# One shared transposed block for the two key triangles of the second query block in a sliding-window attention (float32 decoder trunk)

## The chip, the cores and the metric

The kernel runs on one core of a Trainium2 chip. The metric is the device time of one execution in microseconds (us). Four engines compute: TensorE (PE, matrix products and transposes, with PEld for its weight loads), VectorE (DVE), ScalarE (ACT) and GpSimd (POOL). SyncE (SP) and the queues of ACT and POOL start DMA transfers. The engines run on their own instruction streams, in order, and wait for one another through semaphores.

## The reference, cut to what matters

Two layers; each normalises the stream (256 tokens of 1024 channels), makes one wide input projection, runs three token mixers side by side (a state-space scan, a sliding-window attention with sinks, a forgetting attention), projects and gates each, merges, projects out and adds to the stream. The change is in the sliding-window attention:

```python
SWA_HEADS = 16; SWA_KV_HEADS = 4; HEAD_DIM = 64; SWA_WINDOW = 128; SWA_BLOCK = 128
def sliding_window_branch(q, k, v, z, sinks, cos, sin):
    ...                                   # rope on q and k; two query blocks of 128
    scores = jnp.einsum('bnqkgd,bnskd->bnkgqs', qb, kb).astype(jnp.float32) * (HEAD_DIM ** -0.5)
    diff = qi + blk - sj                  # sj runs over the block before and the own block
    band = (diff >= 0) & (diff < SWA_WINDOW)
    mask = band[None] & (key_pos >= 0)
    scores = jnp.where(mask[None, :, None, None], scores, -jnp.inf)
    ...                                   # the sink is one more column of the softmax
    probs = jax.nn.softmax(jnp.concatenate([scores, sink], axis=-1), axis=-1)[..., :-1]
    out = jnp.einsum('bnkgqs,bnskd->bnqkgd', probs.astype(v.dtype), vb)
    return out.reshape(b, s, SWA_HEADS * HEAD_DIM) * jax.nn.silu(z)
```

With a window of 128 and blocks of 128, query i of the second block sees key j of the block before if j > i, and key j of its own block if j <= i. The two sets of places (i, j) are the two triangles of one 128x128 square, and together they fill it once.

## The kernel before, in words

Products of the wide projections are made in float32r from weights split into a high and a low part: ACT rounds the high part (line 291), DVE subtracts for the low part (line 292), and PE multiplies (line 106). The weight pieces stream through six raw buffers and six split buffers; at most four split parts are held ahead. So the bulk of PE's work is dense products, and the mixers are fitted between them.

The order of PE's work is written by the program itself. Each mixer is a generator. Where it has to wait for other engines, it yields a number of microseconds of PE work (`D_SOFT = 7.0` after the scores, `D_SOFT2 = 3.0` between the two halves of the transposes, `D_EVAC = 3.0` after them). At the end of each dense unit (8 weight tiles against 256 tokens, or a token block against up to 512 columns) the function `pump` looks for generators whose time has come, by a planner's clock, and lets them issue their next step. Steps thus fall on the ends of dense units. The instructions of the other engines are put in order by the scheduler of the tile framework.

Sliding attention: one generator `swa_quad` for each of the four key-value groups of a layer, with four query heads each. It calls `attn_quad`, which the forgetting attention (`fox_quad`) uses too. For a quad, PE makes the scores; DVE adds the mask and takes the row minimum (line 615); ACT takes the exponential with the row sum (line 621); DVE scales each row (line 633). A quad holds two tiles `pp` of [128, 2 heads, 384]: columns 0 to 127 are the first query block, columns 128 to 383 the second query block with its two key blocks. Then PE transposes twelve 128x128 blocks (line 647, recorded at line 110), three for each head, into PSUM tiles of four blocks, ACT copies each tile to SBUF (line 652), and PE multiplies by the values. Only one quad is between its scores and the end of its transposes at a time (`tokens["pp"]`), and the value products of two quads are made together. A state-space group (`ssd_group`) begins when no quad of the sliding attention is left: `yield lambda: not any(m[2] == 1 for m in waiting)`; its first step starts a DMA of decay sums (line 808). The projection of the attention's output begins with `drain`, which runs all steps of that branch that are left.

GpSimd adds the rotated halves of queries and keys (lines 565 and 566), starts the DMAs that add the two parts of a product in SBUF (`dma_sum`, line 492), and masks the bias of the forgetting attention with `affine_select` (line 991). That bias arrives by a DMA that ACT starts (line 984), and its two buffers are shared with the values of the sliding attention.

Of the kernel before, what the change touches and what calls it, by code (L numbers as in the profile page):

```python
# [14 lines left out]
ALU = mybir.AluOpType  # L15

P = 128
S = 256
# [6 lines left out]
D_SOFT, D_SOFT2, D_EVAC, D_SSD, D_SSD2 = 7.0, 3.0, 3.0, 8.0, 4.0  # L25
D_K, D_Q, D_QK, D_G0, D_FOX, D_BDMA, D_BIAS, D_BC, D_SSD3 = 6.0, 5.5, 2.0, 8.0, 0.0, 4.0, 2.6, 5.5, 1.0
D_GN1, D_GN2, D_CUM, D_H, D_M = 8.0, 13.5, 12.0, (4.8, 6.4), 5.0
BUDGET = 1.35
T_PP, T_SSD, T_BIAS = 1, 1, 1
N_RAW, N_SPLIT = 6, 6  # L30
AHEAD = 4
WARM = 7
# [15 lines left out]
def hybrid_trunk(  # L48
# [5 lines left out]
    nc = tc.nc  # L54
# [11 lines left out]
    def T(tag, shape, dtype=F32, bufs=None):  # L66
        count[0] += 1
        return sb.tile(shape, dtype, tag=tag, name=f"{tag}_{count[0]}",
                       bufs=bufs if bufs is not None else BUFS.get(tag, 1))
# [8 lines left out]
    def pmx():  # L78
        return PS("mx", 5)
# [5 lines left out]
    gtt = nc.gpsimd.tensor_tensor  # L85
# [14 lines left out]
    def mm(o, a, b, **kw):  # L100
        n = b.free_size()
        if a.dtype == F32R:
            clock["t"] += max(0.094, n / 2350.0)
        else:
            clock["t"] += max(0.2, n / 587.0) * (0.5 if a.free_size() == 64 or a.shape[0] == 32 else 1.0)
        nc.tensor.matmul(o, a, b, **kw)  # L106

    def transpose(o, a, i):
        clock["t"] += 0.109
        nc.tensor.transpose(o, a, i)  # L110
# [74 lines left out]
    for j in range(2):  # L185
# [6 lines left out]
                            pattern=[[1, P]], channel_multiplier=-1)  # L192
# [3 lines left out]
                            pattern=[[1, P]], channel_multiplier=-1)  # L196
# [9 lines left out]
                            compare_op=ALU.is_ge, fill=NEG, base=0,  # L206
                            pattern=[[-1, P]], channel_multiplier=1)
    nc.gpsimd.affine_select(out=wmask[:, 0:P], in_=wmask[:, 0:P],
                            compare_op=ALU.is_ge, fill=NEG, base=-1,
                            pattern=[[1, P]], channel_multiplier=-1)  # L210
# [7 lines left out]
    def bc(ap, axis, n):  # L218
        s = list(ap.shape)
        s.insert(axis, n)  # L220
        return ap.unsqueeze(axis).to_broadcast(s)
# [204 lines left out]
    for l in range(L):  # L426
        y = Layer()
# [151 lines left out]
    def u_bq(y, g):  # L579

        def done(held):
            q = T("qt", [P, 2, S])
            add_rotated(q, held)
            launch(1, swa_quad(y, g, q), D_Q)
        return rotated(y, done)

    def attn_quad(y, last, products, biases, nsink, v, vcols, sz, gated, scored=lambda: None):

        yield Half("pp")
        pair = y.pair
        if y.values:
            yield Half(lambda: y.values[0] is not None)
            y.values.pop()()
        pps = [T("pp", [P, 2, 3 * P]) for _ in range(2)]
        nm = T("nm", [P, 8], bufs=2)
        sums = T("sums", [P, 8], bufs=2)
        blocks = ((0, slice(0, P)), (1, slice(P, 3 * P)))  # L600

        scs = [pmx() for _ in range(4)]

        def score(p, i, b):
            return scs[2 * p + i][:, b * P:P + 2 * P * b]

        products(score)
        for p in range(2):
            pp = pps[p]
            ps_ = slice(4 * p, 4 * p + 4)  # L610
            ns = None if nsink is None else nsink(p)
            for i in range(2):
                for b, sl in blocks:
                    e = 4 * p + 2 * i + b
                    nc.vector.tensor_tensor_reduce(  # L615
                        out=pp[:, i, sl], in0=score(p, i, b), in1=biases(p, i, b), scale=-0.125,
                        scalar=1.0e30 if ns is None else ns[:, i:i + 1],
                        op0=ALU.add, op1=ALU.min, accum_out=nm[:, e:e + 1])
                for b, sl in blocks:
                    e = 4 * p + 2 * i + b  # L620
                    act(pp[:, i, sl], pp[:, i, sl], AF.Exp, scale=-1.0, bias=nm[:, e:e + 1],  # L621
                        accum_out=sums[:, e:e + 1])
            if nsink is not None:
                es = T("es", [P, 4], bufs=2)
                tt(es.rearrange("p (i b) -> p i b", i=2), nm[:, ps_].rearrange("p (i b) -> p i b", i=2),
                   bc(ns, 2, 2), op=ALU.subtract)
                act(es, es, AF.Exp)
                tt(sums[:, ps_], sums[:, ps_], es, op=ALU.add)
            rs = T("rsum", [P, 4], bufs=4)
            nc.vector.reciprocal(rs, sums[:, ps_])  # L630
            for i in range(2):
                for b, sl in blocks:
                    ts(pp[:, i, sl], pp[:, i, sl], rs[:, 2 * i + b:2 * i + b + 1], 0.5,  # L633
                       op0=ALU.mult, op1=ALU.mult)
        yield D_SOFT
        scored()

        order = [(0, 0), (0, 1), (1, 0), (1, 1), (0, 2), (1, 2),
                 (2, 0), (2, 1), (2, 2), (3, 0), (3, 1), (3, 2)]
        at = {hb: (n // 4, n % 4 * P) for n, hb in enumerate(order)}  # L640
        pTs = []
        for n, (h, b) in enumerate(order):
            if n == 6:
                yield D_SOFT2
            if n % 4 == 0:
                pt = pmx()
            transpose(pt[:, n % 4 * P:(n % 4 + 1) * P], pps[h // 2][:, h % 2, b * P:(b + 1) * P], ident)
            if n % 4 == 3:
                if n == 3:
                    two = T("L4", [P, 2, 512])  # L650
                pT = T("L2", [P, 512]) if n == 11 else two[:, n // 4, :]
                act(pT, pt, AF.Copy)  # L652
                pTs.append(pT)
        yield D_EVAC
        tokens["pp"] += 1

        def products_with_values(bank):
            py = bank()
            for p in range(2):
                for b, o in ((0, 0), (1, P)):  # L660
                    for i in range(2):
                        n, c = at[2 * p + i, 2 * b]
                        mm(py[64 * i:64 * i + 64, S * p + o:S * p + S], v[:, b, vcols(p, i)],
                           pTs[n][:, c:c + S - o], start=(b == 0), stop=(b == 1))
            return py


        pair.append((gated, products_with_values, sz))
        if len(pair) == 2:
            quads = pair[:]  # L670
            pair.clear()

            def values():
                for py, (_, _, own) in zip([f(bank) for (_, f, _), bank in zip(quads, (pmx, pmm))], quads):
                    o = own()
                    tt(o, py.rearrange("p (u s) -> p u s", u=2), o, op=ALU.mult)
            if not last:
                y.values.append(None)
            gates = lambda: all(g() for g, _, _ in quads)
            yield Half(gates) if last else gates  # L680
            if last:
                values()
            else:
                y.values[0] = values

    def swa_quad(y, g, q):
        yield lambda: 1 in y.sz

        def products(score):
            for b in range(2):  # L690
                for c in range(2):
                    for h in range(4):
                        r = slice(32 * h, 32 * h + 32)
                        mm(score(h // 2, h % 2, b), q[r, c, b * P:(b + 1) * P], y.kT[r, (h - g) % 4, c, 0:(b + 1) * P],
                           start=(c == 0), stop=(c == 1))

        yield from attn_quad(
            y, g == 3, products, lambda p, i, b: wmask[:, P:2 * P] if b == 0 else wmask,
            lambda p: y.nsink[:, 4 * g + 2 * p:4 * g + 2 * p + 2], y.bv,
            lambda p, i: slice(64 * g, 64 * g + 64),  # L700
            lambda: y.sz[1][:, 2 * g:2 * g + 2, :], lambda: (1, 2 * g + 1) in y.zdone)


    def logits(y, t, i, p):
# [273 lines left out]
    def fox_quad(y, j):  # L978
# [26 lines left out]
        def scored():  # L1005
            tokens["bias"] += 1

        yield from attn_quad(y, j == 6, products, lambda p, i, b: bs[p][:, i, P * b:P + 2 * P * b], None, y.cv,
                             lambda p, i: slice(P * (j + p) + 64 * i, P * (j + p) + 64 * i + 64),
                             lambda: y.sz[2][:, j:j + 2, :], lambda: (2, j + 1) in y.zdone, scored)  # L1010
# [188 lines left out]
    for y in layers:  # L1199
# [10 lines left out]
        def cols(c0, n=256):  # L1210
            return sub([(0, w[:, c0:c0 + n])], n)
# [39 lines left out]
        if l == 0:  # L1251
            v, cv0, cv1 = cols(C_BV), cols(C_CV), cols(C_CV + 256)
# [8 lines left out]
        else:  # L1261
            cv0, v = cols(C_CV, 512), cols(C_BV)
# [87 lines left out]
    with tc.manual_schedule(engines={ENG.PE, ENG.DVE, ENG.Activation, ENG.Pool}):  # L1350
# [11 lines left out]
        p = pmx()  # L1362
# [93 lines left out]
        for i in range(2):  # L1456
# [4 lines left out]
        v = T("sm", [P, 8])  # L1461
        nc.vector.tensor_reduce(v[:, 0:2], ss.rearrange("p (t j) -> p t j", t=2), axis=mybir.AxisListType.X,
                                op=ALU.add)
# [50 lines left out]
```

## Time and profile before

| | |
|---|---|
| median of 3 runs | 821.57 us (821.18 to 821.93) |
| the profiled execution, its own time | 820.72 us |
| its span, first to last instruction | 819.0 us |
| mean granted TensorE clock | 0.999 |
| PE, PEld busy | 808.4 us (99%), 721.2 us (88%) |
| DVE busy | 671.5 us (82%) |
| ACT busy | 547.6 us (67%) |
| POOL busy | 172.6 us (21%) |

The table's busy times are shares of the whole span. The time outside the span is 1.72 us. Instructions of a helper all carry the helper's line: products line 106, transposes line 110. In the profile's names "x6" is a count, "<-" names what ended a wait, and tiles are called by their tags (`mm` and `mx` are PSUM tiles).

### The profile page before, as it was taken

Reading aid. Unit: us, or ns where it says so; the run is one execution under the profiler, and the core shown is the slowest. Engines: PE = TensorE matmul, PEld = TensorE weight load, DVE = VectorE, ACT = ScalarE, POOL = GpSimd, SP = SyncE. Lnnn points to the kernel's source line nnn. Section 1 sums busy time; section 2 is a strip of 40 time slices with the busy share of each in tenths; the row PEclk is TensorE's granted clock in tenths of the full one; section 3 lists DMA queues with packets and bytes.
Section 4 is the critical chain, followed back from the end, with each engine's and each line's share of the span. In section 5 each row is a group of like instructions: output and inputs, shape, how many; then the busy total and the mean of one; then the engine's idle time right before and its main releaser. Section 6 shows DMA issues by size and latency. Waiting matters only on the chain.

```text
span 819.0 us, 15070 instructions
## 1 busy us (share of the span) xinstructions
PE 808.4 (99%) x5242; PEld 721.2 (88%) x5242; DVE 671.5 (82%) x1468; ACT 547.6 (67%) x1186; POOL 172.6 (21%) x232
## 2 busy tenths in 40 slices
PE   8999999999999999999999999999999999999996
PEld 8998988888888988888999898889888889888896
DVE  6879899888998787965786989988899878787665
ACT  7777878775776767543666777886567767684452
POOL 3066113130210001030005621314004210102100
PEclk9999999999999999999999999999999999999999
DMA  9897869797865554866689787869868565467632
GB/s 312 278 261 193 211 187 256 190 233 214 232 206 157 180 168 148 276 208 205 221 265 265 186 222 206 228 179 259 243 206 231 155 181 163 137 208 265 206 104 77
DMA packets 141653, 170.35 MB, mean 208 GB/s; under 512 B 9314, under 2 KB 110298, under 8 KB 141578
## 3 DMA queue, kind: packets, MB, share of 16 engines
q1 hardware_dynamic: 114960, 140.53, 54.8%
q0 software_dynamic: 12928, 12.63, 9.5%
q10 hardware_dynamic: 13690, 16.24, 6.5%
q8 instruction: 41, 0.67, 0.3%
q14 instruction: 34, 0.28, 0.1%
HBM read 154.63 MB, written 2.16 MB: 191 GB/s over the span
## 4 chain that ended last, share of the span: by engine, by line
PE 85%; DVE 4%; DMA 4%; ACT 4%; issue 2%; POOL 0%; SPq 0%; ACTq 0%; DVEq 0%; POOLq 0%
PE mm L106 75%; PE mx L106 7%; PE mx L110 3%; DMA L<-cumd 2%; DVE lo L292 1%; ACT hi L291 1%; DVE L L781 1%; ACT pp L621 1%; DMA L<-L 1%; DMA raw<-in_w_in_dram 1%; DMA bias<-cumd 1%; ACT L L778 0%; ACT L L490 0%; DVE L L830 0%; POOL bias L991 0%
## 5 line engine op out<-in xcount | busy, mean ns | idle before, releaser
L292 DVE TENSOR_TENSOR lo<-raw,hi 128x1024 fp32r<-128x1024 f32 (+2 forms) x276 | 310.5, 1144 | 53.2 <-ACT hi L291 50.5
L106 PE MATMUL mm<-L,hi 128*128 128x512 f32 x1056 | 353.2, 386 | 0.0
L106 PE MATMUL mm<-hi,L 128*128 128x512 f32 (+2 forms) x1232 | 323.3, 351 | 0.1
L291 ACT ACTIVATE hi<-raw 128x1024 fp32r<-128x1024 f32 (+2 forms) x276 | 263.9, 981 | 57.2 <-PE mm L106 45.2
L106 PE MATMUL mm<-L,lo 128*128 128x256 f32 x1056 | 266.6, 273 | 0.0
L106 PEld LDWEIGHTS mm<-hi,L 128*128 128x128 f32 x1232 | 216.9, 190 | 24.1 <-issue 1.3
L106 PEld LDWEIGHTS mm<-L,hi 128*128 128x128 f32 x1056 | 194.5, 190 | 26.4 <-issue 3.2
L106 PE MATMUL mm<-lo,L 128*128 128x512 f32 (+2 forms) x616 | 213.8, 349 | 1.8 <-DVE lo L292 1.8
L106 PEld LDWEIGHTS mm<-L,lo 128*128 128x128 f32 x1056 | 202.1, 191 | 5.5
L106 PEld LDWEIGHTS mm<-lo,L 128*128 128x128 f32 x616 | 116.3, 190 | 14.1 <-DVE lo L292 2.6
L492 POOL DMA_DIRECT2D L<-L x68 | 59.4, 925 | 184.5 <-ACT L L491 151.3
L621 ACT ACTIVATE pp<-pp,nm 128x128 f32<-128x128 f32 (+1 forms) x128 | 56.5, 442 | 30.8 <-DVE nm L615 30.7
L991 POOL TENSOR_SCALAR_AFFINE_SELECT bias<-bias 128x128 f32<-128x128 f32 x64 | 34.6, 592 | 93.5 <-DMA bias<-cumd 92.7
L781 DVE SCALAR_TENSOR_TENSOR L<-L,vec,L 128x255 f32<-128x255 f32 (+2 forms) x96 | 46.2, 481 | 2.2 <-ACT L L778 0.5
L490 ACT ACTIVATE L<-mm 128x256 f32<-128x256 f32 x84 | 31.6, 376 | 15.9 <-PE mm L106 14.2
L1025 ACT ACTIVATE L<-L 128x512 f32<-128x512 f32 x24 | 15.1, 629 | 31.6 <-DVE L L1022 27.2
L633 DVE TENSOR_SCALAR pp<-pp,rsum 128x128 f32<-128x128 f32 (+1 forms) x128 | 32.5, 319 | 0.5
L492 POOL DMA_DIRECT2D qt<-L x16 | 14.5, 990 | 81.9 <-ACT qt L491 40.4
L877 DVE SCALAR_TENSOR_TENSOR L<-L,L 128x256 f32<-128x256 f32 x48 | 21.4, 449 | 8.6 <-ACT L L876 8.3
L652 ACT ACTIVATE L<-mx 128x512 f32<-128x512 f32 x48 | 26.8, 595 | 1.5 <-PE mx L110 1.5
L1070 POOL TENSOR_TENSOR L<-L,L 128x512 f32<-128x512 f32 x8 | 12.8, 1598 | 68.4 <-DVE L L1069 68.4
L912 POOL TENSOR_TENSOR sm<-sm,mhalf 128x4 f32<-128x4 f32 x8 | 8.1, 1019 | 90.5 <-DVE sm L909 90.5
(197 smaller groups left out, 841.8 us busy)
## 6 DMA issues: line engine op xcount, KB each, us to landing
raw<-in_w_in_dram SPq DMA_DIRECT2D x191, 512.0 KB, 4.7
raw<-in_w_proj_dram SPq DMA_DIRECT2D x48, 512.0 KB, 5.3
L<-L POOLq DMA_DIRECT2D x72, 128.0 KB, 5.0
raw<-in_w_out_dram SPq DMA_DIRECT2D x16, 512.0 KB, 5.1
bias<-cumd ACTq DMA_DIRECT2D x16, 256.0 KB, 3.4
L<-cumd ACTq DMA_DIRECT2D x8, 512.0 KB, 5.9
L<-in_gate_bias_dram ACTq DMA_DIRECT2D x12, 256.0 KB, 5.9
qt<-L POOLq DMA_DIRECT2D x16, 128.0 KB, 5.6
```

The costliest lines, as they stand in the source:

```text
L106: nc.tensor.matmul(o, a, b, **kw)
L110: nc.tensor.transpose(o, a, i)
L291: keep(act)(hi, src, AF.Copy)
L292: keep(tt)(lo, src, hi.bitcast(F32), op=ALU.subtract)
L490: act(halves(lo), ordered(p[:, S:2 * S]), AF.Copy)
L492: nc.gpsimd.dma_start(out, lo, accum_op=ALU.add)
L621: act(pp[:, i, sl], pp[:, i, sl], AF.Exp, scale=-1.0, bias=nm[:, e:e + 1], accum_out=sums[:, e:e + 1])
L633: ts(pp[:, i, sl], pp[:, i, sl], rs[:, 2 * i + b:2 * i + b + 1], 0.5, op0=ALU.mult, op1=ALU.mult)
L652: act(pT, pt, AF.Copy)
L781: stt(a[:, s:S], x_[:, 0:S - s], y.vec[:, 16 * j + u:16 * j + u + 1], a[:, s:S], op0=ALU.mult, op1=ALU.add)
L877: stt(o, th, 1.0, o, op0=ALU.add, op1=ALU.mult)
L991: nc.gpsimd.affine_select(out=bias[:, i, dst], in_=bias[:, i, src], compare_op=ALU.is_ge, fill=NEG, base=0, pattern=[[-1, P]], channel_mul ...
```

## The change: what it does

In the sliding attention alone (`window=True`), GpSimd adds the own block's triangle onto the previous block's triangle in `pp`, once for each of a quad's two tiles. The row scaling covers 128 columns instead of 256 for the second query block. PE transposes eight blocks instead of twelve, four in each half, and ACT copies two tiles instead of three. After each copy GpSimd takes the shared block of two heads apart with two `affine_select` operations of 128x(2x128): one writes the own block's triangle into the tile `own`, the other blanks the rest of the shared block in place. The value products stay as they were, in number and shape. The delay between the scores and the first transposes is 9.0 (`D_FOLD`) instead of 7.0 in the planner's clock.

```diff
+D_FOLD = 9.0
...
-    def attn_quad(y, last, products, biases, nsink, v, vcols, sz, gated, scored=lambda: None):
+    def attn_quad(y, last, products, biases, nsink, v, vcols, sz, gated, scored=lambda: None, window=False):
...
             nc.vector.reciprocal(rs, sums[:, ps_])
+            if window:
+                gtt(pp[:, :, P:2 * P], pp[:, :, P:2 * P], pp[:, :, 2 * P:3 * P], op=ALU.add)
             for i in range(2):
-                for b, sl in blocks:
+                for b, sl in ((0, slice(0, P)), (1, slice(P, 2 * P))) if window else blocks:
                     ts(pp[:, i, sl], pp[:, i, sl], rs[:, 2 * i + b:2 * i + b + 1], 0.5,
                        op0=ALU.mult, op1=ALU.mult)
-        yield D_SOFT
+        yield D_FOLD if window else D_SOFT
         scored()
 
-        order = [(0, 0), (0, 1), (1, 0), (1, 1), (0, 2), (1, 2),
-                 (2, 0), (2, 1), (2, 2), (3, 0), (3, 1), (3, 2)]
+        if window:
+            order = [(h, b) for h in range(4) for b in range(2)]
+        else:
+            order = [(0, 0), (0, 1), (1, 0), (1, 1), (0, 2), (1, 2),
+                     (2, 0), (2, 1), (2, 2), (3, 0), (3, 1), (3, 2)]
...
-            if n == 6:
+            if n == len(order) // 2:
                 yield D_SOFT2
...
                 act(pT, pt, AF.Copy)
                 pTs.append(pT)
+                if window:
+                    if n == 3:
+                        own = T("L2", [P, 512])
+                    k = n // 4
+                    both = pT.rearrange("p (h b q) -> p b h q", h=2, b=2)[:, 1, :, :]
+                    nc.gpsimd.affine_select(out=own[:, k * S:(k + 1) * S].rearrange("p (h q) -> p h q", h=2), in_=both,
+                                            compare_op=ALU.is_ge, fill=0.0, base=0,
+                                            pattern=[[0, 2], [1, P]], channel_multiplier=-1)
+                    nc.gpsimd.affine_select(out=both, in_=both, compare_op=ALU.is_ge, fill=0.0, base=-1,
+                                            pattern=[[0, 2], [-1, P]], channel_multiplier=1)
+                    at.update({(h_, 2): (2, h_ * P) for h_ in (2 * k, 2 * k + 1)})
+        if window:
+            pTs.append(own)
         yield D_EVAC
...
-            lambda: y.sz[1][:, 2 * g:2 * g + 2, :], lambda: (1, 2 * g + 1) in y.zdone)
+            lambda: y.sz[1][:, 2 * g:2 * g + 2, :], lambda: (1, 2 * g + 1) in y.zdone, window=True)
```

## The prediction, made before the changed kernel was run

> **What bounds the kernel now.** I read the page's busy times first, then PE's waits, then the four stretches of the sliding attention (two in each layer), then the chain of work there.
>
> ```profile
> span 819.0 us, 15070 instructions
> PE 808.4 (99%) x5242; PEld 721.2 (88%) x5242; DVE 671.5 (82%) x1468; ACT 547.6 (67%) x1186; POOL 172.6 (21%) x232
> ```
> ```profile
> PE mm L106 <- DVE lo L292: 1.8, 2, 1.2
> PE mx L110 <- POOL ident masks.py:199: 1.5, 1, 1.5
> PE mx L106 <- ACT hi L1389: 0.5, 2, 0.3
> ```
> ```profile
> 66.00:112.00 46.00, 46.00 (x375) 42.02 (x375) 42.06 (x119) 37.58 (x103) 16.72 (x21) 1.00 0.78 207
> 112.00:160.00 48.00, 48.00 (x352) 42.00 (x349) 44.14 (x118) 38.31 (x99) 10.93 (x14) 1.00 0.73 194
> 457.00:503.00 46.00, 46.00 (x374) 42.08 (x375) 41.38 (x117) 37.20 (x103) 16.74 (x20) 1.00 0.76 204
> 503.00:553.00 50.00, 49.82 (x364) 43.35 (x361) 46.12 (x123) 38.84 (x102) 11.49 (x15) 1.00 0.73 195
> ```
>
> In the third fence the columns are the stretch, its length, then busy us (and count) of PE, PEld, DVE, ACT and POOL. PE is busy 99% of the span and waits 3.8 us in total; only 1.8 us of that lies in the body of the kernel, both times for the low half of a weight split on DVE. So an instruction taken from PE's stream should be worth its full pitch. DVE is the next engine: in the four stretches it is busy 42.06 + 44.14 + 41.38 + 46.12 = 173.7 of 190 us, so 16.3 us are free. ACT has 38 free, POOL 134.
>
> ```profile
> 66.39 1.52 PE mx L106 x32
> 67.92 8.06 PE mm L106 x48
> 75.97 0.66 PE mx L110 x6
> 76.63 5.24 PE mm L106 x32
> 81.87 0.66 PE mx L110 x6
> 82.53 5.56 PE mm L106 x48
> 88.09 1.52 PE mx L106 x32
> 135.65 1.52 PE mx L106 x32
> 156.91 1.45 PE mx L106 x16
> ```
>
> This is the chain of work, in order of time, for the first quad: scores, three dense units, six transposes, two units (5.24 us, so 2.62 each), six transposes, two units, the next quad's scores. It is PE alone: nothing here waits for the softmax. The last two rows are the fourth quad's scores and its value products.
>
> **The change part by part.** *PE.* Six transposes take 0.66 us, 0.109 each (the modelled duration below, 273 ns, overlaps with the next one). Four of twelve go, in four quads and two layers: 32 x 0.109 = 3.5 us. Value products and scores stay. Since PE waits for nothing else here, I take the whole 3.5 us as gain, before new waits.
>
> ```profile
> L110 PE MATMUL mx<-ident,pp 128*128 128x128 f32 x192 | 26.3, 273 | 0.0
> L633 DVE TENSOR_SCALAR pp<-pp,rsum 128x256 f32<-128x256 f32 x64 | 22.5, 352 | 0.0
> L633 DVE TENSOR_SCALAR pp<-pp,rsum 128x128 f32<-128x128 f32 x64 | 18.4, 287 | 0.5
> L652 ACT ACTIVATE L<-mx 128x512 f32<-128x512 f32 x48 | 26.8, 595 | 1.5 <-PE mx L110 1.5
> ```
>
> *ACT and DVE savings.* Eight of 48 copies of 595 ns go, 4.8 us of ACT. Half of the 64 wide scalings (those of the sliding attention) become narrow: 32 x (352 - 287) = 2.1 us of DVE. Both are hidden under PE; worth nothing by themselves, but DVE's 2.1 us offset what follows.
>
> *GpSimd's additions.* Sixteen adds of 128x(2x128), the size of the rotation adds; 32 masks of 128x(2x128), twice the bias masks.
>
> ```profile
> L565 POOL TENSOR_TENSOR qt<-L,L x8: 732/1200/2735, 57.9 to 468.0; 128x256 f32<-128x256 f32 x8
> L991 POOL TENSOR_SCALAR_AFFINE_SELECT bias<-bias x64: 284/465/2453, 135.2 to 671.6; 128x128 f32<-128x128 f32 x64
> L204 POOL MEMSET wmask<- 128x256 f32 x1 | 0.3, 302 | 0.0
> L198 POOL MEMSET L<- 128x128 f32 x1 | 0.2, 194 | 0.0
> ```
>
> An add takes 0.73 to 2.74 us (minimum, median, maximum stand before the times). A mask of 128 columns takes 0.28 at least; the second 128 columns cost a memset 0.11, so I estimate 0.40 at least for 256 and, doubling the median, 0.93 as usual. One quad then gives GpSimd 2 x 1.2 + 4 x 0.93 = 6.1 us, eight quads 49 us, in stretches with 134 us free. It fits. What it costs others is the question.
>
> *DVE beside GpSimd.* The same DVE form, with and without a GpSimd add beside it, and the masks beside a weight split:
>
> ```profile
> 80.19 1.10 POOL L566 TENSOR_TENSOR qt<-L,L 128x256 f32<-128x256 f32 x1
> 80.63 0.95 DVE L877 SCALAR_TENSOR_TENSOR L<-L,L 128x256 f32<-128x256 f32 x1
> 83.73 0.43 DVE L877 SCALAR_TENSOR_TENSOR L<-L,L 128x256 f32<-128x256 f32 x1 [0.81 <-ACT L L876]
> 135.17 2.51 POOL L991 TENSOR_SCALAR_AFFINE_SELECT bias<-bias 128x128 f32<-128x128 f32 x4 [4.46 <-DMA bias<-cumd]
> 136.22 1.31 DVE L292 TENSOR_TENSOR lo<-raw,hi 128x1024 fp32r<-128x1024 f32 x1
> 137.88 1.21 DVE L292 TENSOR_TENSOR lo<-raw,hi 128x1024 fp32r<-128x1024 f32 x1
> ```
>
> One add delays a DVE instruction with two SBUF inputs by 0.95 - 0.43 = 0.52 us; a mask beside a split costs it 1.31 - 1.21 = 0.10. Sixteen adds: 8.3 us of DVE; 32 masks at 0.10: 3.2. Less the 2.1 saved: 9.4 us more DVE work into 16.3 free us, busy 96% instead of 91%. Splits are held up to four parts ahead, so most of it should not reach PE. Bounds: nothing (all beside DVE instructions that don't mind, and the 1.8 us of waits gone too), or the full durations as in the second rival. I take 1.0 us, half again the 1.8 us that PE already waits for DVE.
>
> The Trainium skill speaks against the change here: "SBUF — State Buffer", section "SBUF: two separate sides", says that GpSimd and a DVE instruction with two SBUF inputs share a port pair as an exclusive lock, held for the whole instruction, the other blocked fully. For the add the rows agree nearly (0.52 of 0.73); for the mask they don't (0.10 of 0.28 or more). By the page the sum would be the second rival's.
>
> *The fold's wait.* The scaling now waits for GpSimd's add, behind which the DMA starts of line 492 queue on POOL. The planner allows 9 instead of 7 us before the transposes; those fall on unit ends 2.62 us apart, so in practice one unit later. That covers an add of 0.73 to 2.74 us. Cost nothing; without that cover up to 2 us a quad.
>
> *The masks' wait.* Value products wait for copy and masks.
>
> ```profile
> 153.69 1.08 ACT L652 ACTIVATE L<-mx 128x512 f32<-128x512 f32 x2
> ```
>
> In the fourth quad the two copies end at 154.77, 2.1 us before the value products at 156.91 (above). With one copy less they end about 0.5 sooner, so 2.6 us remain for two masks of 0.8 to 1.9. Cost nothing.
>
> *The quads' spacing.* A quad takes 88.09 - 66.39 = 21.7 us now. With the first wait one unit longer (+2.62) and four transposes less (-0.44) it takes up to 2.2 more. Walking all four through the unit ends I get 2.1, 2.1, -0.7 and 1.9: the last values come 5.4 us later, about 162.3 instead of 156.9. That alone costs PE nothing, dense units fill it.
>
> Sum: -3.5 + 1.0 = -2.5 us on the profiled execution's 820.72 us: 818.2. The median of the runs shown, 821.57, lies 0.85 above that execution, so I forecast a median of 819.1.
>
> **The rivals.** *Later state-space start, slower.* The state-space groups begin when the last quad has finished, and both waits for DVE in the body end chains that begin there:
>
> ```profile
> 159.47 8.88 DMA L<-cumd
> 168.58 4.83 DMA bias<-cumd
> 174.21 1.65 POOL bias L991 x2
> 175.86 5.93 DMA L<-L
> 182.93 1.14 DVE lo L292
> 551.15 8.88 DMA L<-cumd
> 574.06 1.15 DVE lo L292
> ```
>
> After the last values the decay sums are fetched (8.88 us), ACT starts the bias DMA behind them, GpSimd's masks wait for that, a DMA that adds a convolution's parts queues behind the masks, DVE's taps wait for it, and the weight split behind those releases PE: 1.2 us late in the first layer. The chain has no slack. If its order stays and it starts s later, while PE gets there 16 x 0.109 = 1.75 us sooner, each layer loses s + 1.75, and the total is -3.5 + 2(s + 1.75) = 2s: slower from s = 0. With s = 5.4 in both layers +10.8, a median of 832.4; in one layer -3.5 + 7.15 = +3.65, 825.2. For it: both layers show the chain. Against: the queues are ordered anew, and work that starts later may then stand behind that split instead of ahead of it. Chance 0.23.
>
> *DVE becomes the bound, slower.* If every addition holds DVE for its whole shortest duration: 16 x 0.73 + 32 x 0.40 - 2.1 = 22.4 us into 16.3, so 6.1 us over, and -3.5 + 6.1 = +2.6: 824.2. It decides from an average of 0.22 us per mask on (then 16.3 is full). For it: the stretch 503 to 553 has 3.9 us free only. Against: the 0.10 measured. Chance 0.16. This is the result that the Trainium skill's rule in "SBUF — State Buffer" gives.
>
> *The gain turns into a wait for the masks.* A bias mask has taken 2.45 us (the row above). If one of the two does so, they need 2.45 + 0.93 = 3.4 us where 2.6 are free: 0.8 us at each of the four pairs of quads, 3.2 in all, and -2.5 + 3.2 = +0.7: 822.3, within what can be told from no change. Against: the usual mask leaves slack. Chance 0.14.
>
> *More than forecast.* The re-ordered chain lets both 1.8 us waits go and DVE costs nothing: -5.3, a median of 816.3. Chance 0.11.
>
> **How the numbers follow.** Forecast 0.36, rivals 0.23, 0.16, 0.14, 0.11. A measurement of this kernel tells about 0.2%, 1.6 us, from no change. Faster by more: 0.36 + 0.11 = 0.47. Within: 0.14. Slower: 0.23 + 0.16 = 0.39. The forecast's own range is 818.1 (no new wait) to 820.0. The range over the cases goes from 815.6, a little under the best case, to 828.0, between the chain in one layer and in both; it leaves out about 0.05 below and 0.13 above.
>
> **What would show it.** Right: 160 transposes of pp, 40 copies, PE's waits in the body at 3 us or less, DVE some 9 us busier, the last values of the first layer near 162. The chain rival shows as PE waiting for the split of DVE near 181 and 573 for several us; DVE's as many waits for splits between 66 and 160; the masks' as PE waiting for POOL at the value products. Wrong altogether, if PE gained less than 3.5 us without a wait that can be named.

## The result, and the profile after

The changed kernel takes 830.94 us (median of four executions, 828.25 to 834.78) where the kernel before takes 821.75 us beside it (821.18 to 821.97): a ratio of 1.0121, 95% interval 1.0098 to 1.0144. It is 9.2 us slower; 2.5 us faster was forecast. All lines named below are those of the changed kernel, which from line 28 on stand one or more further down than before; each run below has its own line numbers in the same way.

The profiled execution took 830.75 us. Its page, span and busy times:

```profile
span 829.0 us, 15065 instructions
...
PE 811.0 (98%) x5210; PEld 721.2 (87%) x5210; DVE 681.8 (82%) x1468; ACT 547.8 (66%) x1178; POOL 207.4 (25%) x280
```

PE has its 32 transposes less, GpSimd its 48 instructions more, and DVE's busy time is up by 10.3 us (671.5 before). PE's waits in the body of the kernel (engine, line, what for: us in total, times, longest):

```profile
PE mm L107 <- ACT L L492: 3.4, 2, 1.9
PE mx L107 <- DVE nm L616: 3.1, 2, 1.8
PE mm L107 <- DVE lo L293: 1.8, 2, 1.3
PE mx L107 <- DVE L L866: 1.2, 2, 1.0
```

The first two are new. L492 is ScalarE's eviction of a product: it copies the sums out of PSUM, and only then is that bank (buffer) free for PE's next product. L616 is the reduction over the scores, which also frees one. Both lie in the sliding attention's stretches (same columns as in the prediction; the column before the last two is the granted clock):

```profile
66.00:112.00 46.00, 43.21 (x338) 39.38 (x337) 40.49 (x105) 33.19 (x94) 22.79 (x29) 1.00 0.70 183
112.00:160.00 48.00, 46.14 (x324) 39.69 (x323) 44.09 (x122) 35.33 (x93) 16.91 (x24) 0.96 0.69 183
457.00:503.00 46.00, 43.62 (x330) 39.28 (x329) 38.76 (x101) 31.88 (x91) 25.44 (x30) 0.96 0.71 180
503.00:553.00 50.00, 48.62 (x348) 42.33 (x348) 47.83 (x129) 38.21 (x100) 19.72 (x26) 1.00 0.72 196
```

PE was busy 189.8 of these 190 us; now 181.6. In the first and third, DVE is *less* busy than before (40.49 against 42.06): it is not saturated there, it is late and then waits too.

How the first stall comes about, from the timeline (start, duration, engine, line; in brackets the idle time before and what ended it):

```profile
74.22 1.02 POOL L633 TENSOR_TENSOR pp<-pp 128x256 f32<-128x256 f32 x1 [2.10 <-ACT pp L622]
78.86 3.28 POOL L566 TENSOR_TENSOR qt<-L,L 128x256 f32<-128x256 f32 x1 [0.85 <-DVE L L556]
82.11 1.70 POOL L567 TENSOR_TENSOR qt<-L,L 128x256 f32<-128x256 f32 x1
83.77 1.75 POOL L493 DMA_DIRECT2D L<-L  x2
...
88.58 0.42 ACT L897 ACTIVATE L<-L 128x256 f32<-128x256 f32 x1 [3.49 <-DMA L<-L]
...
96.97 0.34 DVE L616 CUSTOM_DVE_ANT_0 pp<-mx,wmask,nsink 128x128 f32<-128x128 f32 x1
...
101.81 0.48 PE L107 MATMUL mm<-L,hi 128*128 128x512 f32 x1 [1.46 <-ACT L L492]
```

L493 starts the transfers that add a product's low part to its high part; GpSimd starts them, behind its rotation adds (L566, L567). They start at 83.77. ScalarE waits 3.49 us for one of them (L897, the gate's activation) and then has weight splits and evictions to make up. DVE needs these splits and comes late to the second quad's scores (96.97), ScalarE's exponentials and the evictions behind them come later still, and at 100.35 PE finds no PSUM bank. In the kernel before, the two rotation adds took 2.73 and 1.10 us (here 3.28 and 1.70) and the transfers started at 81.25. ScalarE came to the same activation (85.68) without a wait, and to the one ahead of it with 0.71 us. The scores' reductions began 5.3 us sooner; 2.4 of that is the longer delay, since PE makes these scores at 90.4 instead of 88.0:

```profile
81.25 1.74 POOL L492 DMA_DIRECT2D L<-L  x2
...
83.28 0.42 ACT L876 ACTIVATE L<-L 128x256 f32<-128x256 f32 x1 [0.71 <-DMA L<-L]
...
85.68 0.42 ACT L876 ACTIVATE L<-L 128x256 f32<-128x256 f32 x1
...
91.68 0.34 DVE L615 CUSTOM_DVE_ANT_0 pp<-mx,wmask,nsink 128x128 f32<-128x128 f32 x1
```

### The profile page after: what moved, and what is told of

The parts are those of the page before. It is cut to its first block, busy times and chain, and to the rows that moved or that the text cites. A ratio compares the mean times of both kernels' runs of the same rounds, so it can differ in the third digit from the quotient of the medians.

```text
span 829.0 us, 15065 instructions
## 1 busy us (share of the span) xinstructions
PE 811.0 (98%) x5210; PEld 721.2 (87%) x5210; DVE 681.8 (82%) x1468; ACT 547.8 (66%) x1178; POOL 207.4 (25%) x280
## 4 chain that ended last, share of the span: by engine, by line
PE 76%; DVE 12%; issue 4%; DMA 4%; ACT 3%; POOL 1%; ACTq 0%; DVEq 0%; POOLq 0%
PE mm L107 67%; PE mx L107 6%; PE mx L111 3%; DVE lo L293 3%; DVE L L802 2%; DMA L<-L 2%; DMA L<-cumd 2%; DVE pp L616 2%; ACT hi L292 1%; DVE pp L636 1%; ACT L L799 1%; DVE L L556 0%; DVE L L866 0%; POOL qt L567 0%; DVE sums L629 0%
## 5 line engine op out<-in xcount | busy, mean ns | idle before, releaser
L293 DVE TENSOR_TENSOR lo<-raw,hi 128x1024 fp32r<-128x1024 f32 (+2 forms) x276 | 311.8, 1148 | 53.3 <-ACT hi L292 50.0
L107 PEld LDWEIGHTS mm<-lo,L 128*128 128x128 f32 x616 | 116.3, 190 | 11.6
L493 POOL DMA_DIRECT2D L<-L x68 | 59.6, 905 | 114.1 <-ACT L L492 103.8
L493 POOL DMA_DIRECT2D qt<-L x16 | 13.9, 887 | 87.9 <-ACT qt L492 84.5
L933 POOL TENSOR_TENSOR sm<-sm,mhalf 128x4 f32<-128x4 f32 x8 | 11.4, 1430 | 85.6 <-DVE sm L930 85.6
L897 ACT ACTIVATE L<-L 128x256 f32<-128x256 f32 x48 | 19.8, 414 | 13.9 <-DMA L<-L 7.4
```

The source lines that it names most:

```text
L293: keep(tt)(lo, src, hi.bitcast(F32), op=ALU.subtract)
L493: nc.gpsimd.dma_start(out, lo, accum_op=ALU.add)
L897: act(th, o, AF.Tanh, scale=0.5)
```

## The experiments

Each run stands beside executions of the kernel before on the same chip; "before" is their median, given where it changes. Times are medians; a profile shows one execution, and where that one lies far from the median its own time is given. Theories: **queue** (the addition holds up what stands behind it on GpSimd, and the scaling waits for it), **port** (GpSimd's reading and writing holds DVE), **delay** (the 9.0 and the order that follows), and later **transfer** (L493's sums come late).

**e1: the kernel before with the delay alone.**

```diff
+D_FOLD = 9.0
-        yield D_SOFT
+        yield D_FOLD if nsink is not None else D_SOFT
```


> The kernel before, with nothing changed but the sliding attention's delay between scores and transposes, 9.0 instead of 7.0. Theory queue (the GpSimd add waits for the softmax at the head of GpSimd's queue, DMA starts behind it come late, ScalarE and then TensorE wait): no GpSimd work is added, so 820 to 823 us. Theory port (GpSimd's data work holds VectorE): the same, 820 to 823. Theory delay (the later steps themselves, and the order that follows from them, cost the time): 826 to 831, most of the loss.

832.75 us (830.90 to 836.82), before 821.11: ratio 1.0144, 1.0106 to 1.0182. The delay alone costs 11.6 us, more than the whole change. ScalarE's wait for the transfer and the first stretch:

```profile
88.86 0.42 ACT L877 ACTIVATE L<-L 128x256 f32<-128x256 f32 x1 [5.15 <-DMA L<-L]
```
```profile
66.00:112.00 46.00, 42.61 (x320) 38.44 (x319) 38.00 (x103) 33.09 (x96) 18.46 (x19) 0.93 0.71 178
```

No GpSimd work was added, and the stall is of the same kind, only longer. So GpSimd's additions are not needed for it. But this run is not the change's delay alone: with twelve transposes the longer delay falls on other unit ends, and PE's order is neither that of the kernel before nor the changed one's. In it the first rival's mechanism does appear. PE waits for splits near 192 and 589, 4.3 us in all, each at the end of a chain that begins with a transfer of decay sums (9.66 and 10.47 us).

**e2: the addition on DVE.**

```diff
-                gtt(pp[:, :, P:2 * P], ..., op=ALU.add)
+                tt(pp[:, :, P:2 * P], ..., op=ALU.add)
```


> The changed kernel with the add of the two triangles on VectorE instead of GpSimd; the masks stay on GpSimd. Theory queue: nothing waits for the softmax in GpSimd's queue any more, 819 to 823 us. Theory port: 16 adds of 0.42 us on VectorE take the place of 16 holds of about 0.6 us, so only some of the loss goes, 825 to 829. Theory delay: 828 to 832, as the changed kernel.

832.17 us (830.41 to 834.15), ratio 1.0135, 1.0111 to 1.0159: nothing is won by taking it off GpSimd. The queue theory, for which this should have been 819 to 823, falls. On DVE the add takes 0.42 us, about the 0.52 that I had put down for an add beside it on GpSimd.

**e3, e4, e5: masks, addition, or both left out.** Without the masks the value products read the shared block.

```diff
e3: -  own = T("L2", ...) and the two affine_select
e4: -  gtt(pp[:, :, P:2 * P], ..., op=ALU.add)
e5: -  both
```


> The changed kernel without the affine_selects: the value products read the shared block unmasked for both triangles (this part of the computation is left out). Theory queue: the fold is the cause, 826 to 831 us. Theory port: 32 masks hold VectorE for 0.1 to 0.4 us each, so 3 to 6 us come back, 823 to 828. Theory delay: 828 to 832.

> The changed kernel without the add of the two triangles; the masks stay (the own block's keys are left out of the sum). Theory queue: 818 to 821 us. Theory port: 16 x 0.6 us of VectorE come back and the masks' stay, 820 to 825. Theory delay: 828 to 832.

> The changed kernel, delay 9.0, without the add and without the masks (own block's keys left out, the shared block used for both): what is left is the savings of TensorE, ScalarE and VectorE and the longer delay. Theory delay (the first four runs: the delay alone cost 11.6 us): delay minus savings, 824 to 829 us, TensorE waiting near 100 or 124 us as in the changed kernel. Theory GpSimd (fold 5 us and masks 2.4 us on top of each other make the loss): 818 to 822.

e3: 828.53 us (1.0093, 1.0066 to 1.0120). e4: 825.86 us (1.0053, 1.0038 to 1.0068). e5: 823.27 us, before 821.72 (1.0015, 1.0000 to 1.0029). The addition is worth 5 us with or without the masks (830.94 - 825.86; 828.53 - 823.27), the masks 2.4 to 2.6. Yet e5 is e1 with twelve transposes cut to eight a quad and shorter scalings, and it stands 9.5 us below e1: taken this way the parts do not add up, and the delay is no fixed price.

**e6: the addition cut to two columns a head; e7: the change with a delay of 7; e8: e5 with a delay of 7.**

```diff
e6: -  gtt(pp[:, :, P:2 * P], pp[:, :, P:2 * P], pp[:, :, 2 * P:3 * P], op=ALU.add)
    +  gtt(pp[:, :, P:P + 2], pp[:, :, P:P + 2], pp[:, :, 3 * P - 2:3 * P], op=ALU.add)
e7, e8: -D_FOLD = 9.0   +D_FOLD = 7.0
```


> The changed kernel with the add cut to two columns for each head (the rest of the sum is left out): the wait in GpSimd's queue and its place stay, the data work goes. Theory queue: as the changed kernel, 829 to 833 us. Theory port: as without the fold, 824 to 827. Theory delay: the fold's wait or work are not the cause, only the delay is; 826 to 832.

> The changed kernel with the delay put back to 7.0, add and masks on GpSimd as they are. Theory delay: the loss goes, 818 to 823 us. Theory GpSimd (queue or port): the loss stays, 826 to 832, with TensorE waiting for the transposes' input as well, since the add is no longer covered.

> Delay 7.0, no add, no masks (the same parts left out as in the run without both): only the savings of the change. Both theories: TensorE's 32 transposes of 0.109 us less, 817 to 819 us; if the order of the queues, made anew, costs by itself, 820 to 826.

e6: 824.82 us (823.26 to 830.22). The place in GpSimd's queue and the wait are kept, the data work is gone, and the time is e4's. The recorded orders of PE, DVE and ACT are the same in e3 to e6 and the changed kernel, so the 5 to 6 us are the addition's data work and no other order. e7: 833.25 us, the old delay does not help, and its profile names why:

```profile
PE mm L107 <- DVE lo L293: 3.1, 2, 1.6
PE mx L111 <- DVE pp L636: 2.4, 2, 1.5
...
PE mx L111 <- DVE sums L629: 1.4, 3, 0.5
```

The transposes now wait for the scaling: the 2 us that the delay of 9 adds are needed. e8: 820.95 us (819.45 to 822.30), 0.9989, 0.9977 to 1.0001: with no addition, no mask and no longer delay, the saved transposes give 0.8 us and not 3.5.

With e8 and e5 the parts do add up, each step taken on the one before: the savings alone -0.8 us (e8 against the kernel before), the longer delay +2.3 (e5 against e8), the addition and the masks +7.7 (the changed kernel against e5), 9.2 in all. In the full change the same delay gains 2.3 (against e7).

**e9, e10: e5 with an idle addition of constants, on GpSimd and on DVE.**

```diff
+            if window:
+                gtt(sa, w3, w3, op=ALU.add)      # e10: tt
```


> The kernel with the savings only at a delay of 9 us (no addition on the softmax, no masks; the value products read the shared block; 823.3 us), to which GpSimd gets, at the place of the addition, an addition of two constants of the same 128x256 into a scratch tile that nobody reads and nothing waits for. Port theory (GpSimd's reading holds VectorE, wherever the addition stands): the 5 to 6 us that the addition has cost come back: 828 to 829. Chain theory (the cost is that the scaling, the transposes and the next quad come later behind the addition): 823 to 824. Queue theory: 823 to 824.

> As the run before, with the idle addition on VectorE (128x256, some 0.6 us each, 16 of them, 9.6 us of VectorE's work), again read by nobody. If VectorE's time by itself is what is short in these stretches (17 us free in four of them), 828 to 831, as with the addition in the chain on VectorE (832.2 with masks, less 2.5 for the masks: 829.7). If only the place in the chain counts: it stands ahead of the scaling in VectorE's order, so this cannot be told from the chain; 823 to 824 would say that neither VectorE's time nor that order matters.

826.97 us and 825.90 us (before 821.36), but neither tells what it was made for: with no input to wait for, the sixteen additions ran in the kernel's first 35 us. In e9 they held up the start: PE stands 3.3 us behind e5's at 40 us, part of it lost to a lower clock (a granted clock of 0.83 between 10 and 20 us, 1.00 in e5).

e10 lost nothing there. Its PE and GpSimd orders are e5's, and so are DVE's and ACT's between 40 and 820 us. But one GpSimd add near 82 us took 1.78 us where it took 0.72 in e5, and the chain of the first section followed. First e5's timeline and first stretch (an execution of 821.95 us), then e10's (827.39 us):

```profile
81.93 0.72 POOL L567 TENSOR_TENSOR qt<-L,L 128x256 f32<-128x256 f32 x1
82.59 2.64 POOL L493 DMA_DIRECT2D L<-L  x3
...
87.21 0.42 ACT L885 ACTIVATE L<-L 128x256 f32<-128x256 f32 x1 [1.78 <-DMA L<-L]
```
```profile
66.00:112.00 46.00, 45.07 (x352) 41.32 (x351) 40.74 (x117) 35.66 (x97) 17.68 (x20) 1.00 0.77 203
```
```profile
82.62 1.78 POOL L567 TENSOR_TENSOR qt<-L,L 128x256 f32<-128x256 f32 x1
84.35 2.63 POOL L493 DMA_DIRECT2D L<-L  x3
...
89.53 0.42 ACT L889 ACTIVATE L<-L 128x256 f32<-128x256 f32 x1 [4.11 <-DMA L<-L]
```
```profile
66.00:112.00 46.00, 43.95 (x334) 40.04 (x333) 39.05 (x106) 33.94 (x99) 18.95 (x20) 0.96 0.73 194
```

So, in these two executions, transfers that start 1.8 us later go with a first stretch that lacks 2.05 us of PE instead of 0.93. This gave the transfer theory.

**e11, e12: the first key block's scaling moved from DVE to ScalarE, in the changed kernel and in the one before.**

```diff
+                    if window and b == 0:
+                        act(pp[:, i, sl], pp[:, i, sl], AF.Copy, scale=hs[:, 2 * i:2 * i + 1])
+                        continue
```


> The whole change, with one thing more: in the sliding attention the scaling of the first key block (32 in all, 0.287 us each) goes from VectorE to ScalarE, for a VectorE instruction of 128x4 a tile (16 of some 0.07 us): VectorE has 8 us less to do, ScalarE some 8 us more, of the 38 us that it has free in these stretches. If VectorE's time is what the addition and the masks cost, it comes back: 823 to 826 instead of 831. If it is GpSimd's queue or the wait for it, 830 to 832. If ScalarE's evictions behind the scaling are what PE waits for, slower: 832 to 835.

> The kernel before the change, with the same move of the first key block's scaling to ScalarE in the sliding attention. There VectorE keeps up (PE waits 1.8 us for it in all), so no gain is to be had from its time: 820 to 823. More than 2 us slower would say that the move itself costs (ScalarE's evictions come later), and the run with the whole change is then read against that.

835.56 us (1.0169, 1.0149 to 1.0189) and 823.69 us (1.0030, 1.0018 to 1.0041). Relief for DVE at ScalarE's cost makes both slower, the changed kernel by 4.6 us. PE's waits in e11:

```profile
PE mm L107 <- DVE lo L293: 4.1, 2, 2.0
PE mm L107 <- ACT L L492: 2.8, 4, 1.0
PE mm L107 <- ACT qt L492: 2.1, 2, 1.6
```

PE's waits for ScalarE's evictions are now 4.9 us in six, where the changed kernel has 3.4 in two. It says that ScalarE has no room in this chain either; whether DVE's time was the price it cannot say.

**e13, e14: e5 with an idle addition that reads the softmax's third block**, so that it runs where the change's addition runs, and nobody waits for it.

```diff
+            if window:
+                gtt(sa, pp[:, :, 2 * P:3 * P], pp[:, :, 2 * P:3 * P], op=ALU.add)   # e14: tt
```


> The kernel with the savings only at a delay of 9 us (no addition on the softmax, no masks; 823.3 us), with a GpSimd addition of 128x256 a tile that reads the third key block after the exponentials and writes a scratch tile: its place in time is that of the changed kernel's addition, nobody waits for it. Port theory: GpSimd's reading holds VectorE as in the changed kernel, 826 to 829 (with the addition in the chain and no masks it was 828.5). Transfer theory: the addition delays the transfers behind it on GpSimd by 0.7 to 1.5 us, so part of the loss comes also, 824 to 827. If it is only the chain from the addition to the scaling that costs: 823 to 824.

> As the run before, with that idle addition on VectorE (0.42 us measured where it stood alone, 16 of them, 6.8 us). Port or VectorE's time: 826 to 829. Transfer theory (GpSimd's queue is free of it): 823 to 824.5.

828.67 us (825.86 to 829.49) and 827.60 us (823.14 to 830.67), before 821.61: 5.4 and 4.3 us over e5. e13 equals e3, which has the same add inside the chain and the wait for it (828.53). PE's, DVE's and ACT's orders are the same in e13, e3 and e5. So the wait costs nothing that these runs can tell; what costs is an add of this size, at this place, on either engine. (With the add on DVE, in e14 as in e2, DVE's and ACT's instructions also stand in another order in places, so e13 is the cleaner of the two.) e14 missed what the transfer theory gave it, 823 to 824.5: GpSimd's queue is free of the addition, and yet its two rotation adds take 4.19 and 1.71 us and the transfers start at 83.70, as late as in the changed kernel. The price comes in whole stalls. The profile of e14 is that of its fastest execution (823.14 us); it has one stall in the first layer and none in the second:

```profile
88.75 0.42 ACT L888 ACTIVATE L<-L 128x256 f32<-128x256 f32 x1 [3.89 <-DMA L<-L]
...
479.61 0.42 ACT L888 ACTIVATE L<-L 128x256 f32<-128x256 f32 x1 [0.56 <-DMA L<-L]
```
```profile
66.00:112.00 46.00, 43.23 (x330) 39.38 (x329) 39.50 (x113) 33.49 (x94) 18.58 (x19) 0.96 0.73 190
...
457.00:503.00 46.00, 46.00 (x358) 42.20 (x357) 41.70 (x116) 35.79 (x101) 19.29 (x20) 1.00 0.81 210
```

Where ScalarE waits 3.89 us for the transfer the stretch lacks 2.8 us of PE, where it waits 0.56 it is full.

**e15, e16: without L493's transfers, the changed kernel and the one before.** Out of 84 products' sums the low part is missing.

```diff
-        nc.gpsimd.dma_start(out, lo, accum_op=ALU.add)
```


> The whole change, without the transfers of line 493 that add the low part of a product to the high part (all 84 left out, the low part is missing in the result). Transfer theory: ScalarE no longer waits near 86 us, the scores of the second quad are in time, and the loss goes: 820 to 824. Port theory: the addition still takes 0.5 us of VectorE a tile and the masks theirs; 827 to 831.

> The kernel before the change without the same transfers. TensorE waits for nothing there, so 817 to 821.5: what it gains is what the transfers cost in the kernel before (the chains to the weight splits near 183 and 574, 1.8 us, and the end). The difference of the two runs is then the cost of the change without these transfers: near -2.5 if transfers carry the loss, +6 or more if not.

822.56 us (820.89 to 826.35) and 818.30 us (818.02 to 819.18). The kernel before gains 3.3 us, the changed one 8.4: of the change's 9.2 us, about 5 hang on these transfers and 4.3 do not (PE's, DVE's and ACT's orders are those of the changed kernel in e15, and of the kernel before in e16). e15's first stretches and its waits in the body:

```profile
66.00:112.00 46.00, 45.85 (x357) 42.01 (x356) 40.58 (x116) 36.65 (x100) 10.81 (x14) 1.00 0.56 172
112.00:160.00 48.00, 46.47 (x335) 40.37 (x334) 45.50 (x118) 35.73 (x93) 11.34 (x16) 1.00 0.56 168
```
```profile
PE mx L107 <- DVE nm L616: 2.9, 2, 1.5
```

The wait for evictions is gone. What is left is the wait for L616, with DVE busy 45.50 of 48 us.

**e17, e18: e5 and e1 without those transfers.** (The edit is e15's.)

> The savings only at a delay of 9 us (no addition on the softmax, no masks; 823.3 us with the transfers), without the transfers that add the low part of a product. If the transfers ate the saved transposes: 818.3 - 3.5 = 814.8, up to 816.5 with one small wait. If something else in the new order does (the value products' place, the waits for nm near 122 us): 817.5 to 820.

> The kernel before the change with the delay of 9 us alone (832.75 us with the transfers), without those transfers. If the delay costs through the transfers that come late: 818 to 821, near the 818.3 of the kernel before without them. If the delay costs by itself (later value products, a later start of what follows): 826 to 830.

e17: 818.22 us (818.17 to 818.47), the same as e16. e18: 821.19 us (820.06 to 824.90). The medians side by side, each with and without the transfers:

| | with | without |
|---|---|---|
| kernel before | 821.6 | 818.30 |
| before, delay 9 (e1, e18) | 832.75 | 821.19 |
| savings only, delay 9 (e5, e17) | 823.27 | 818.22 |
| whole change (after, e15) | 830.94 | 822.56 |

In the order of e1 and e18 the delay costs 11 us with the transfers and 2.9 without, 1.7 of them waits for the splits at the end of the state-space chain. Addition and masks cost 7.7 with and 4.3 without, in one and the same order of PE, DVE and ACT. And the saved transposes bring nothing even in e17, where PE's waits are small:

```profile
PE mx L107 <- DVE nm L616: 1.9, 2, 1.0
...
PE mx L107 <- ACT hi L1398: 0.7, 2, 0.4
```

## Why the prediction was wrong, point by point

*The sum.* Forecast: savings -3.5, delay 0, addition and masks +1.0. Measured, each on top of the one before: -0.8, +2.3, +7.7. The largest error is the term for what DVE's extra work does to PE; the savings and the delay were wrong too.

*The counts were right.* There are 160 transposes of the softmax and eight copies less, the add takes 0.72 us at least and the masks 0.40 at least, as estimated:

```profile
L111 PE MATMUL mx<-ident,pp x160: 272/273/307, 78.6 to 705.5; 128*128 128x128 f32 x160
...
L633 POOL TENSOR_TENSOR pp<-pp x16: 721/733/1027, 71.1 to 548.8; 128x256 f32<-128x256 f32 x16
L667 POOL TENSOR_SCALAR_AFFINE_SELECT L<-L x16: 404/834/1511, 84.9 to 564.8; 128x256 f32<-128x256 f32 x16
```

*"DVE beside GpSimd", busy time: the sum right, by luck in part.* Forecast +9.4 us, measured +10.3. Addition and masks alone were to be 8.3 + 3.2 = 11.5; they are 12.5 (681.8 against e5's 669.3), and 8.6 without the transfers (e15 against e17). But the addition adds 5.0 us (e3 against e5) to 7.3 (the changed kernel against e4), less than forecast, and the masks 5.2 (e4 against e5) to 7.5 (the changed kernel against e3), or 0.16 to 0.23 us each instead of 0.10. That 0.10 came from a row that was read wrongly. It merges four masks; the last of them, beside the split, began after the split did and took 1.27 us where a mask takes 0.28 at least. So there the mask waited for DVE, and the lock that the prediction found missing for masks shows in its own row.

*"Most of it should not reach PE. I take 1.0 us": the step that failed.* Addition and masks cost 4.3 us without the transfers and 7.7 with them. The 16.3 free us of DVE were counted over 190 us, as if any of them could be used. They cannot: the add falls into the softmax of one quad, and what follows it there is a chain from DVE through ScalarE to the PSUM banks, in which little was late before and little had slack (ScalarE's waits for these transfers were 0.9 us at most). Splits held "four parts ahead" protect the dense products, and PE did not stall for these first; it stalled for banks.

*"I take the whole 3.5 us as gain": wrong.* With no addition and no masks 0.8 us came out at the old delay (e8), and none at the new one without the transfers (e17 against e16; the delay's cost stands against the 3.5 there). Of e17's missing 3.5 us, waits for L616 are 1.9, which the kernel before did not have. In e8, PE's waits sum to 6.1 us against 3.8 in the kernel before; the largest are for the same weight splits, near 184 and 576, 2.5 us instead of 1.8:

```profile
PE mm L107 <- DVE lo L293: 2.5, 2, 1.3
```

The rest I could not assign. A gain under 3.5 us without a wait that can be named was the prediction's own sign of being wrong altogether, and for this rest it holds.

*"The fold's wait. Cost nothing": right for the wait, wrong for its cover.* e13 shows no price for waiting on the add, and e7 that the cover is needed. But the cover, two more us of delay, was costed at nothing because "dense units fill it". With the savings alone it costs 2.3 us (e5 against e8). The forecast had moved the last value products of the first layer by 5.4 us, to 162.3; in the profile they start at

```profile
170.13 1.52 PE L107 MATMUL mx<-L,bias 128*64 128x256 f32 x16
```

so 13.2 us later than before. e17, in which PE has the same order and waits 1.0 us on the way, starts them at 164.26. So about 6.4 us are the plan's, near the forecast, and most of the other 6.8 are stalls (4.6 us of waits before that point) and the clock that they cost (1.7 us, last section).

*Queues.* I asked whether the transfers would stand behind the add on GpSimd, and answered by the planner's delay. The step missed was one transfer further: what waits for the landing. In the kernel before ScalarE hardly waits there, but its row was on the page of waits, and only PE's were read:

```profile
ACT L L876 <- DMA L<-L: 2.5, 3, 0.9
```

Three waits under 1 us for such a transfer say that it lands just as its reader comes. In the changed kernel the same row has 7.4 us in two waits, the longer of 3.9.

*The rivals.* The later state-space start (832.4 or 825.2) has the measured time inside its span but not its mechanism, so that is chance: the waits for splits near 181 and 573 do not appear, and L293's two waits lie at 103 and 501. With the delay alone (e1) the waits at the end of that chain do appear. The masks' wait at the value products does not appear. The nearest is "DVE becomes the bound" (824.2): its additions do hold DVE, and e3 to e6, e13 and e14 show that this costs. Its masks, too, came near the average from which it was to decide (0.16 to 0.23 us measured; 0.22 there, 0.21 by its own terms). But it reckoned a saturated engine and waits for splits, where DVE stays under 96% busy in every stretch and the price is paid in stalls of 2 to 3 us through a third engine. This is also where the Trainium skill's rule, "SBUF — State Buffer", section "SBUF: two separate sides", stands: a DVE instruction with two SBUF inputs and a GpSimd one that reads SBUF exclude each other for a whole instruction. The trace bears it out on a very small instruction, which unhindered takes 0.15:

```profile
99.34 0.73 POOL L633 TENSOR_TENSOR pp<-pp 128x256 f32<-128x256 f32 x1 [5.07 <-ACT es L628]
```
```profile
99.37 0.71 DVE L629 TENSOR_TENSOR sums<-sums,es 128x4 f32<-128x4 f32 x1
101.93 0.15 DVE L629 TENSOR_TENSOR sums<-sums,es 128x4 f32<-128x4 f32 x1
```

That instruction stands in the softmax's chain itself. An add on DVE costs about as much, though (e2, e14), so what seems to count is the half microsecond a tile and not who spends it; the runs do not separate the two further.

*What is open.* That the transfers carry half of the loss is shown by taking them out. Whether they do it by starting late, by landing late among the weights' transfers, or by the room that they take on GpSimd and the DMA engines isn't separated, since leaving them out removes all three. Why e10 is always above e5's median, with the same order in the body, is open as well. With that much hanging on one or two microseconds, differences of 2 to 3 us between two runs (the masks' 2.4 and the delay's 2.3 among them) shouldn't be read as the price of a part in another kernel.

## What to carry to other kernels

A PE that is 99% busy shows what it does, not how much slack the chains behind it have: before adding even half a microsecond to a chain, follow it through the other engines up to the buffer that PE needs next, and look for the places that just make it, such as a transfer that lands right when its reader comes. They show, if at all, as short waits of an engine that is not the bottleneck. A cover (a longer delay, a later unit) is a change of its own, and its price depends on the order that it falls into: here 11.6 us in the kernel before and 2.3 with the savings. Try it by itself, in the kernel in which it is to stand. And an instruction saved on a full engine is a gain only if what feeds that engine can come as much sooner.

## What the runs showed of the hardware

I had not expected that a stall of PE costs more than its length. After the 1.80 us wait that ends at 126.90 the granted clock falls to half (2-us windows of the changed kernel, the clock third from the end):

```profile
126.90 0.28 PE L107 MATMUL mx<-tri,da 128*16 128x128 f32 x1 [1.80 <-DVE nm L616]
```
```profile
126.00:128.00 2.00, 1.04 (x7) 0.60 (x8) 2.00 (x13) 1.47 (x7) 0.00 (x0) 0.87 0.03 10
128.00:130.00 2.00, 2.00 (x9) 1.37 (x8) 2.00 (x11) 2.00 (x10) 0.72 (x1) 0.50 0.00 0
130.00:132.00 2.00, 2.00 (x11) 1.80 (x11) 1.93 (x9) 2.00 (x10) 1.53 (x2) 0.78 0.00 0
```

The missing shares, 0.13 + 0.50 + 0.22 of 2 us each, are 3.4 us at half clock, 1.7 us lost on top of the wait. After the 1.91 us wait near 499 it comes again (0.96 in the third stretch above), so some 3.4 us of the 9.2 are clock. In e5, where no wait in the body is longer than 1.0 us, the first stretch above keeps a clock of 1.00. The length of the wait alone does not decide, though: in e10 a wait of 2.03 us that ends at 496.8 left the clock of its third stretch at 1.00. The Trainium skill, "TensorE: Matmul & The Clock Gate", section "Part 1: The HAM clock gate", gives a window of about 3.4 us for this gate; the length agrees, but here a wait of 1.8 us was enough, about half of the idle window that it names.
